# Softmax minus one-hot on one core: which queue issues the stores of the second rows

## The chip, the cores and the metric

The kernel runs on one core of a Trainium2 chip. The core has five engines with instruction streams of their own: TensorE (PE), VectorE (DVE), ScalarE (ACT), GpSimd (POOL) and SyncE (SP). They meet at semaphores. Data move between HBM and the on-chip memory SBUF by DMAs, which an engine issues and sixteen DMA engines carry out. In this kernel SP and ACT issue DMAs. The profile calls SP's DMA queue q1 and ACT's q10, and marks issues by SPq and ACTq.

The metric is the device time of one execution in microseconds. An execution under the profiler gives a span, from the first to the last instruction, which is a little shorter than the time of a run.

## The reference

The kernel computes the gradient of a cross entropy with respect to the logits: the softmax of each row, minus one at the row's label. There are 8 x 1024 rows of 8192 float32.

```python
logits_max = np.max(logits, axis=-1, keepdims=True)
exp_logits = np.exp(logits - logits_max)
softmax = exp_logits / np.sum(exp_logits, axis=-1, keepdims=True)
...
one_hot[batch_idx, seq_idx, labels] = 1.0
return (softmax - one_hot).astype(np.float32)
```

The logits are read once and the output is written once, 268 MB each way.

## The kernel before

The 8192 rows are cut into 32 blocks of 256. A block holds two rows on each of the 128 partitions (G = 2): partition p has the rows 2p and 2p + 1 of its block, beside each other in memory. In what follows "a row" is the tile of 128 partitions x 8192 float32, one row of each partition. So there are 64 rows, t = 0 to 63; t0 is the first and t1 the second row of a block b, and j = t mod 2 says which one it is. SBUF holds three blocks (SLOTS = 3), each with both rows in place: a row is loaded, worked on where it lies, and stored from there. Block b + 3 goes into the slot of block b.

Each row passes through these steps:

- `load(b)` (lines 101 to 112). The string `LOADS` says in what pieces: blocks 0 to 2 in half tiles ("s"), blocks 3, 4 and 29 to 31 by row ("r"), and blocks 5 to 28 in one piece with both rows ("w"). Each piece waits for the stores of the rows whose place it takes. All loads are issued by SP, but for one half of the pieces of blocks 0 to 2, which ACT issues.
- `row_max(t)`: VectorE takes the negated maximum (TENSOR_REDUCE).
- `exponentials(t)`: ACT computes the exponentials in place and their sum (ACTIVATE X<-X,m).
- `mark(t)`: ACT writes the one-hot of the row as bytes into `hot`, in PSUM, with two activations. `hot` has room for two rows, so the marker of row t + 2 waits until row t is finished (`freed`).
- `finish(t)`: VectorE takes the reciprocal of the sum, then scales the row and subtracts the one-hot bytes, in place (SCALAR_TENSOR_TENSOR).
- `store(t)` (lines 114 to 133): the finished row goes to HBM. `STORES` has "r" for all blocks: one DMA of 4 MB for each row. The last two rows go in halves, the first of them from SP and the second from ACT (lines 117 to 124).

The order of the work is written out by hand in the loop at the end (lines 244 to 279), and each engine runs its instructions in that order. For block b it is: the maximum of t1, finish t0, exponentials of t1, store t0, marker of t0 + 2; then the maximum of the next block's first row, finish t1, exponentials of the next first row, store t1, marker of t1 + 2, and at last `load(b + 3)`. So on ACT's stream the store of a row stands between the exponentials of the row after it and a marker, and waits there for VectorE's `finished[t]`. On SP's stream there is nothing behind the first loads but further loads and, at the very end, the halves of row 62. An engine's stream goes on once a DMA is issued; it doesn't stop until the data have landed, but a wait in it holds back all that stands behind.

All instructions are recorded by the helper `run` (lines 71 to 82), which sets all waits but the last as instructions of their own (line 75) and the last one on the instruction itself. Line 76 is therefore the line of nearly all instructions in the profile, and rows are told apart by engine, operation and tile. A one-piece load waits at line 75 for the store of its slot's first row, and at line 76 for that of the second.

Of the kernel before, what the change touches and what calls it, by code (L numbers as in the profile page):

```python
# [9 lines left out]
SLOTS = 3  # L10
# [7 lines left out]
def kernel(  # L18
# [6 lines left out]
    nc = tc.nc  # L25
# [38 lines left out]
    with tc.tile_critical():  # L64
        sem = tc.alloc_semaphore
        got = [[sem(f"got{i}{q}") for q in range(4)] for i in range(SLOTS)]
        put = [[sem(f"put{i}{q}") for q in range(4)] for i in range(SLOTS)]
# [3 lines left out]
        def run(engine, waits, counter, method, **operands):  # L71

            waits = list(dict.fromkeys(waits))
            for w in waits[:-1]:
                engine.wait_ge(*w)  # L75
            instruction = getattr(engine, method)(**operands)  # L76
            for w in waits[-1:]:
                instruction._wait_ge(*w)
            step = 16 if method == "dma_start" else 1
            instruction.then_inc(counter, step)  # L80
            count[counter.name] = count.get(counter.name, 0) + step
            return counter, count[counter.name]
# [16 lines left out]
        maxed, summed, marked, finished, freed = {}, {}, {}, {}, {}  # L99
# [14 lines left out]
        def store(t):  # L114
            b, j = divmod(t, G)
            stored.setdefault(b, [])
            if t >= T - G:
                for i, cs in enumerate(sides):
                    w = run(
                        nc.sync if t == T - G else nc.scalar, [sides_done[t][i]], put[b % SLOTS][G * j + i],  # L120
                        "dma_start", out=o_b[b, every, one[j], cs], in_=X[every, b % SLOTS, one[j], cs],
                    )
                    stored[b].append(((every, one[j]), w))
                return
            for q, piece in enumerate(PIECES[STORES[b]]):
                ps, js = piece
                if js.stop != j + 1:
                    continue
                w = run(
                    nc.scalar, [finished[t]], put[b % SLOTS][q], "dma_start",  # L130
                    out=o_b[b, ps, js, :], in_=X[ps, b % SLOTS, js, :],
                )
                stored[b].append((piece, w))
# [110 lines left out]
        for b in range(B):  # L244
            t0, t1 = b * G, b * G + 1
            nxt = t1 + 1
            if ORDER[b] == "b":
                if t0 not in maxed:
                    row_max(t0)
                    exponentials(t0)  # L250
                row_max(t1)
                exponentials(t1)
                finish(t0)
                store(t0)
                mark(t0 + G)
                finish(t1)
                store(t1)
                mark(t1 + G)
                if b + SLOTS < B:
                    load(b + SLOTS)  # L260
                continue
# [4 lines left out]
            finish(t0)  # L266
            exponentials(t1)
            store(t0)
            mark(t0 + G)
            ahead = nxt < T and ORDER[b + 1] == "r"  # L270
# [42 lines left out]
```

## Time and profile before

| what | value |
|---|---|
| time of a run, median of 3 | 1248.87 us (1248.83 to 1249.43) |
| span of the profiled execution | 1246.6 us |
| VectorE busy | 1120.2 us, 90% |
| ACT busy | 722.7 us, 58% |
| DMA queues, share of the sixteen engines' span | 51.5% (q10) and 48.3% (q1) |
| HBM read, written | 268.50 MB, 268.44 MB |

Views of the profile are used as follows. The page gives the busy time of each engine, the DMA queues (packets, MB, share of the sixteen engines' span) and the DMA issues (size, and the median us from issue to landing). The waits tell who waited for whom (us in total, times, longest). The chain of waits is followed back from the end of the program, in order of time (start us, us, what). The timeline has start, duration, engine, line, operation, output<-input; a duration with "x2" spans from the first to the last of two instructions, and what stands in brackets is the idle time before it and what ended it. A row of a table by stretches has start:end, length, the busy time of PE, PEld, DVE, ACT and POOL, then PE's clock, the DMA share and GB/s. The DMA view may be limited to a stretch; its packets count where they start, and its issues carry their own time to landing.

### The profile page before, as it was taken

Reading aid. Unit: us, or ns where it says so; the run is one execution under the profiler, and the core shown is the slowest. Engines: PE = TensorE matmul, PEld = TensorE weight load, DVE = VectorE, ACT = ScalarE, POOL = GpSimd, SP = SyncE. Lnnn points to the kernel's source line nnn. Section 1 sums busy time; section 2 is a strip of 40 time slices with the busy share of each in tenths; the row PEclk is TensorE's granted clock in tenths of the full one; section 3 lists DMA queues with packets and bytes.
Section 4 is the critical chain, followed back from the end, with each engine's and each line's share of the span. In section 5 each row is a group of like instructions: output and inputs, shape, how many; then the busy total and the mean of one; then the engine's idle time right before and its main releaser. Section 6 shows DMA issues by size and latency. Waiting matters only on the chain.

```text
span 1246.6 us, 809 instructions
## 1 busy us (share of the span) xinstructions
PE 0.4 (0%) x2; PEld 0.3 (0%) x2; DVE 1120.2 (90%) x208; ACT 722.7 (58%) x257; POOL 2.3 (0%) x7
## 2 busy tenths in 40 slices
PE   0000000000000000000000000000000000000000
PEld 0000000000000000000000000000000000000000
DVE  5999998889988889888898888998889988899995
ACT  2866664556555565465655655556556555566662
POOL 0000000000000000000000000000000000000000
DMA  9999999999999999999999999999999999999998
GB/s 406 413 431 434 437 432 444 435 437 421 433 429 437 443 423 433 434 431 435 430 441 435 422 435 435 434 440 426 432 434 431 433 446 434 422 430 435 429 434 383
DMA packets 15413, 536.98 MB, mean 431 GB/s; under 512 B 1808, under 2 KB 1808, under 8 KB 1840
## 3 DMA queue, kind: packets, MB, share of 16 engines
q10 hardware_dynamic: 9744, 276.89, 51.5%
q1 hardware_dynamic: 5664, 260.05, 48.3%
q14 instruction: 5, 0.04, 0.0%
HBM read 268.50 MB, written 268.44 MB: 431 GB/s over the span
## 4 chain that ended last, share of the span: by engine, by line
DMA 59%; DVE 26%; issue 11%; ACT 3%; DVEq 0%; ACTq 0%; SPq 0%
DMA X<-in_logits_dram 33%; DMA out_dram<-X 26%; DVE X L76 15%; DVE m L76 10%; ACT X L76 2%; DVEq L64 0%; DVE r L76 0%; ACT hot L76 0%; ACT away L76 0%; ACTq L76 0%; DVEq L75 0%; ACTq L308 0%; SPq L64 0%
## 5 line engine op out<-in xcount | busy, mean ns | idle before, releaser
L76 ACT ACTIVATE X<-X,m 128x8192 f32<-128x8192 f32 x64 | 455.8, 7122 | 365.2 <-DVE m L76 365.2
L76 DVE TENSOR_REDUCE m<-X 128x1 f32<-128x8192 f32 x64 | 555.6, 8682 | 105.4 <-DMA X<-in_logits_dram 105.4
L76 DVE SCALAR_TENSOR_TENSOR X<-X,r,hot 128x8192 f32<-128x8192 f32 (+1 forms) x66 | 560.1, 8489 | 3.8 <-ACT hot L76 1.6
L76 ACT ACTIVATE away<-count,word 128x2048 bf16<-128x2048 int16 x64 | 128.1, 2001 | 127.0 <-DVE X L76 127.0
L76 ACT ACTIVATE hot<-away,unit,minus 128x2048 int32<-128x2048 bf16 x64 | 131.9, 2061 | 2.1
L76 ACT ACTIVATION_READ_ACCUMULATOR X<-X,m 128x1 f32 x64 | 11.9, 186 | 0.0
L76 DVE RECIPROCAL r<-s 128x1 f32<-128x1 f32 x64 | 9.8, 153 | 0.0
L76 ACT ACT_TABLE_LOAD x1 | 1.3, 1283 | 5.3 <-issue 5.3
L76 DVE CAST lab_f<-lab_raw 32x256 f32<-32x256 int32 x1 | 0.5, 536 | 2.7 <-DMA lab_raw<-in_labels_dram 2.7
L76 POOL IOTA count<- 128x2048 int16 x1 | 1.8, 1823 | 0.0
L76 DVE TENSOR_TENSOR unit<-unit,part 128x64 f32<-128x64 f32 x3 | 0.7, 225 | 0.1
L76 DVE CAST lab<-hot 128x64 int32<-128x64 f32 x1 | 0.2, 224 | 0.5 <-PE hot L76 0.5
L76 DVE TENSOR_SCALAR part<-minus 128x64 f32<-128x64 f32 x3 | 0.6, 194 | 0.1
L76 PE MATMUL hot<-ident,lab_f 32*128 32x32 f32 x2 | 0.4, 298 | 3.3 <-DVE lab_f L76 3.3
L76 PEld LDWEIGHTS hot<-ident,lab_f 32*128 32x128 f32 x2 | 0.3, 192 | 3.3 <-DVE lab_f L76 3.3
L76 DVE CAST minus<-lab 128x64 f32<-128x64 int32 x1 | 0.2, 195 | 0.0
L76 DVE TENSOR_SCALAR word<-part 128x64 f32<-128x64 int32 x1 | 0.2, 195 | 0.0
L76 DVE TENSOR_SCALAR lab<-lab 128x64 int32<-128x64 int32 x1 | 0.2, 195 | 0.0
L76 DVE TENSOR_SCALAR unit<-minus 128x64 f32<-128x64 f32 x1 | 0.2, 195 | 0.0
L76 DVE TENSOR_SCALAR part<-lab 128x64 int32<-128x64 int32 x1 | 0.2, 194 | 0.0
L76 DVE TENSOR_SCALAR minus<-unit 128x64 f32<-128x64 f32 x1 | 0.2, 194 | 0.0
L76 POOL TENSOR_SCALAR_AFFINE_SELECT ident<-ident 32x32 f32<-32x32 f32 x1 | 0.2, 203 | 0.1
(5 smaller groups left out, 0.5 us busy)
## 6 DMA issues: line engine op xcount, KB each, us to landing
out_dram<-X ACTq DMA_DIRECT2D x62, 4096.0 KB, 30.4
X<-in_logits_dram SPq DMA_DIRECT2D x10, 4096.0 KB, 28.1
X<-in_logits_dram SPq DMA_DIRECT2D x6, 2048.0 KB, 32.6
X<-in_logits_dram ACTq DMA_DIRECT2D x6, 2048.0 KB, 37.1
out_dram<-X SPq DMA_DIRECT2D x2, 2048.0 KB, 12.7
out_dram<-X ACTq DMA_DIRECT2D x2, 2048.0 KB, 11.9
X<-in_logits_dram SPq DMA_DIRECT2D x24, 33.4
lab_raw<-in_labels_dram ACTq DMA_DIRECT2D x1, 64.0 KB, 1.8
```

What stands on the lines that cost most here:

```text
L76: instruction = getattr(engine, method)(**operands)
```

## The change

The stores of second rows (j = 1) of the blocks 0 to 30 are issued by SP in place of ACT. In SP's stream they stand where `store(t1)` is called, which is just ahead of the call of `load(b + 3)`. The stores of first rows stay with ACT, and the halves of the last two rows stay where they were. Waits, sizes, semaphores and the order of all else are the same.

```diff
                 w = run(
-                    nc.scalar, [finished[t]], put[b % SLOTS][q], "dma_start",
+                    nc.sync if j else nc.scalar, [finished[t]], put[b % SLOTS][q], "dma_start",
                     out=o_b[b, ps, js, :], in_=X[ps, b % SLOTS, js, :],
                 )
```

## The prediction

> Names: L(b) is the load of block b, F(b) the store of its first row (j = 0), S(b) the store of its second row (j = 1). A row is 128 x 8192 f32, 4.19 MB; a load in one piece ("w", blocks 5 to 28) is 8.39 MB.
>
> **What bounds the kernel now.** I read the page first, for engines and DMA.
>
> ```profile
> span 1246.6 us, 809 instructions
> PE 0.4 (0%) x2; PEld 0.3 (0%) x2; DVE 1120.2 (90%) x208; ACT 722.7 (58%) x257; POOL 2.3 (0%) x7
> ...
> q10 hardware_dynamic: 9744, 276.89, 51.5%
> q1 hardware_dynamic: 5664, 260.05, 48.3%
> ...
> out_dram<-X ACTq DMA_DIRECT2D x62, 4096.0 KB, 30.4
> ...
> X<-in_logits_dram SPq DMA_DIRECT2D x24, 33.4
> lab_raw<-in_labels_dram ACTq DMA_DIRECT2D x1, 64.0 KB, 1.8
> ```
>
> VectorE is busy 90%, but the two DMA queues (q1 is SP's, q10 ACT's) fill 51.5 + 48.3 = 99.8% of the sixteen engines' time. 536.9 MB in 0.998 x 1246.6 = 1244 us is 0.4316 MB a us: a row takes 9.72 us of the whole DMA, a one-piece load 19.44. A block (two rows in, two out) takes 38.9 us. No shorter time than about 1244 is to be had without moving fewer bytes, and any moment in which both queues are empty is added to the end. So I look only for such moments. By stretches, then by waits:
>
> ```profile
> 198.70:1050.80 852.10, 0.00 (x0) 0.00 (x0) 767.10 (x133) 496.21 (x176) 0.00 (x0) 1.00 1.00 433
> 1050.80:1246.60 195.80, 0.00 (x0) 0.00 (x0) 178.28 (x34) 108.71 (x38) 0.00 (x0) 1.00 0.99 425
> ```
>
> ```profile
> DVE m L76 <- DMA X<-in_logits_dram: 105.4, 26, 8.9
> ...
> SPq L75 <- DMA out_dram<-X: 511.1, 24, 21.6
> ```
>
> The first stretch runs from the issue of L(6) to that of L(28): 22 periods in 852.1 us, 38.73 each, DMA share 1.00 (next to last number). VectorE waits for loads, 105.4 us in all, and SP waits 24 times at line 75 for a store: once for each one-piece load. The chain of waits and the timeline give one period:
>
> ```profile
> 482.00 26.58 DMA out_dram<-X
> ...
> 508.59 33.63 DMA X<-in_logits_dram
> ...
> 559.82 26.10 DMA out_dram<-X
> ...
> 585.94 33.61 DMA X<-in_logits_dram
> ```
>
> ```profile
> 503.58 8.69 DVE L76 TENSOR_REDUCE m<-X 128x1 f32<-128x8192 f32 x1 [4.16 <-DMA X<-in_logits_dram]
> 508.59 38.99 SPq L76 DMA_DIRECT2D X<-in_logits_dram  x2
> 512.37 8.75 DVE L76 SCALAR_TENSOR_TENSOR X<-X,r,hot 128x8192 f32<-128x8192 f32 x1
> 521.15 0.34 ACTq L76 DMA_DIRECT2D out_dram<-X  x1
> 529.82 8.75 DVE L76 SCALAR_TENSOR_TENSOR X<-X,r,hot 128x8192 f32<-128x8192 f32 x1
> 538.60 0.34 ACTq L76 DMA_DIRECT2D out_dram<-X  x1
> 542.25 8.69 DVE L76 TENSOR_REDUCE m<-X 128x1 f32<-128x8192 f32 x1 [3.69 <-DMA X<-in_logits_dram]
> ```
>
> Call the landing of a load A (503.6 here). VectorE then takes the maximum of the new block's first row and finishes the block before it: S is issued at A + 17.6 (521.15), F of the new block at A + 35.0 (538.60). Then VectorE waits for the next landing (542.25). An S takes 26.6 us to land, and its landing releases a load (482.00 + 26.58 = 508.58, issue 508.59). The point to see is what the DMA does between landings:
>
> ```profile
> q1 hardware_dynamic: 144, 8.39, 61.3%
> q10 hardware_dynamic: 178, 5.31, 38.8%
> ```
>
> ```profile
> q10 hardware_dynamic: 81, 2.13, 100.8%
> ```
>
> The first fence is the stretch 510.5 to 542.2: the load moves 8.39 MB, the stores beside it 5.31. The second is 542.3 to 547.2, from the load's last packets to the next load's issue: q10 alone fills the engines. ACT's queue still holds S, with F (538.60) behind it, when S lands and while the next load starts. That backlog is what hides the turn from store to load.
>
> **The change part by part.** *On ACT:* 31 second-row stores go (blocks 0 to 30), 31 x 0.34 = 10.5 us of issue. ACT is busy 58% and the marker behind each store waits for the same VectorE instruction, so I count nothing.
>
> *On SP, the waits:* S(k) stands in front of L(k+3). SP reaches it when L(k+2) is out, waits for VectorE, issues, and goes on to wait for S(k) to land, as it did before. L(k+3) needs S(k) anyway, so the added wait holds up no one-piece load. The row-wise loads (blocks 3, 4, 29 to 31) could start on their first row earlier than S is issued; for them S is queued in front and streams first, so the engines have work and I count nothing.
>
> *On the rings:* this is where the time changes. S(k) now lies in SP's queue behind L(k+2), in order, and ACT's queue holds F alone. Take the landing of L(k+2) as A. At A the queue goes over to S(k); F(k+1) is issued a little before A. Packets of stores are equal (178 for 5.31 MB on q10, some of them completions of no size), so S and F share evenly, and two rows take 2 x 9.72 = 19.4 us. F started no later, so it is done first or at the same time. S lands at about A + 19.4. Now both queues are empty: the next S is at best issued by SP behind the load it has yet to issue, and the next F comes 35 us after A. SP issues L(k+3), which runs alone for 19.4 us. The period is 19.4 + gap + 19.4: the old 38.7 plus the gap.
>
> *The gap* is the landing of the store, the issue of the load, and the time until its packets run on idle engines. No row of before has this turn, so I bound it. The two ends are DMAs issued at the start, on empty engines: the labels' (last row of the first fence) and the first piece of L(0), here the traffic up to its landing and its issue:
>
> ```profile
> DMA packets 150, 3.28 MB, mean 349 GB/s; under 512 B 20, under 2 KB 20, under 8 KB 52
> ...
> q1 hardware_dynamic: 68, 2.10, 58.3%
> q10 hardware_dynamic: 82, 1.18, 29.6%
> ```
>
> ```profile
> X<-in_logits_dram SPq DMA_DIRECT2D x1, 2048.0 KB, 9.9
> ```
>
> The labels: 1.8 us for 0.064 MB, of which 0.15 is data, leaves 1.65. The first load piece on SP: 9.9 us from issue (0.96) to landing. Until then (0.95 to 10.35) the engines moved 3.28 MB, without the labels 3.22, which is 7.5 us of data; 2.4 is left. This is the fixed part of a DMA from issue to landing, and a chain store, load, store pays it once at each turn. I take 2.4, since that DMA is SP's own load with large packets. The dearer end is the start of a load while the other queue runs (508.6 to 512.0, just behind an issue):
>
> ```profile
> q10 hardware_dynamic: 40, 1.31, 89.2%
> ...
> X<-in_logits_dram SPq DMA_DIRECT2D x1, 33.6
> ```
>
> In 3.4 us not one packet of q1 has begun. On engines that have run empty there is nothing to stand behind, so I keep 3.4 as the upper end only. The lower end is 0: F may cover the gap.
>
> The Trainium skill (DMA: Bandwidth & Descriptors, section "Anatomy of one DMA") gives a DMA a fixed cost of about 2.0 us, mostly the receipt of the last write; by it the sum below would be 23 x 2.0 = 46 us instead of 55.
>
> *Does F cover it?* F is issued at 35.0 after its block's landing. At a period of 41.1 that is 6.1 before the next landing, more than the 3.4 that a queue needed to get its turn beside the other one, so F runs when S begins, and S is the last to end. At 38.7 F would be issued only 3.7 before (538.60 to 542.25): too close to call. Once a gap has opened, F is issued earlier still against the landing, and the gap stays.
>
> *How many gaps:* one for each one-piece load, 24. The first, L(5), falls where VectorE has not yet waited long for a load, so first-row stores still come every 35 us without regard to landings and one is likely queued:
>
> ```profile
> 149.25 0.34 ACTq L76 DMA_DIRECT2D out_dram<-X  x1
> ...
> 184.15 0.34 ACTq L76 DMA_DIRECT2D out_dram<-X  x1
> 192.52 8.69 DVE L76 TENSOR_REDUCE m<-X 128x1 f32<-128x8192 f32 x1 [8.41 <-DMA X<-in_logits_dram]
> ```
>
> I count 23. Behind L(28) the loads come in rows: the first row of the next one waits for an F that landed long before, and is queued right behind S, so no gap opens; that stretch, at 0.99 now, stays full.
>
> **The sum.** 23 x 2.4 = 55 us on the profiled 1246.6 gives 1301.8. The median of the runs shown, 1248.87, lies 2.3 above that span, so the forecast is **1304**. With VectorE's wait: 3.7 becomes about 6.1 a period, and at 35.0 us a block VectorE does not take over.
>
> **Rivals.** *(1) The queue does not matter* (not slower). The same bytes run on the same engines; F gets its turn late and is still running when S lands, so the load's start is hidden as now. It decides at 3.4 us: if F is issued less than the time a queue needs for its turn before the load's end, S is ahead by up to two packets on each engine and F outlasts it. For it: 3.7 against 3.4, and load packets, twice as large (144 packets, 16 of them completions, for 8.39 MB), may hold an engine longer. Against: one late turn on one of sixteen engines opens a gap, which then feeds itself. Time: 1246.6 + 2.3 = 1249.
> The Trainium skill speaks for this one (same page, section "Issuing engines are not separate DMA queues"): DMAs of SP and ACT run on the same engines and interleave, and the choice of issuer only saves time on the issuing sequencer. The fences above agree that both queues share the engines (61.3 and 38.8%).
>
> *(2) Half covered.* S is ahead by one packet, and F outlasts it by that: 178 - 16 = 162 packets for 5.31 MB are 0.0328 MB each, on one of sixteen engines 0.0328 / (0.4316 / 16) = 1.2 us. Gap 2.4 - 1.2: 23 x 1.2 = 28, 1276. F's turn would have to come at 4 to 6 us.
>
> *(3) A dear start.* If the 3.4 us belong to any queue that has run empty, the gap is 3.4 and some landing time, say 3.6: 23 x 3.6 = 83, 1332. Against it: the labels' whole trip of 1.8.
>
> *(4) The load keeps its 33.6 us* although it now follows S strictly: the period is 19.4 + 2.4 + 33.6 = 55.4, 23 x 16.7 = 384, 1633. Against it: 33.6 came from sharing (5.31 MB beside it).
>
> *(5) Faster:* at best the 0.2% of DMA time that is idle now, 2.5 us: 1246.
>
> **How the numbers follow.** Forecast 62%, (1) 12, (2) 15, (3) 8, (4) 1, (5) 2. About 0.2% (2.5 us) is what a measurement of this kernel can tell from no change: faster 0.02, same 0.11, slower 0.87. The forecast alone, with the gap at 1.65 to 2.8 (the landings of sixteen engines may spread further), covers 23 x 1.65 = 38 to 23 x 2.8 = 64: 1287 to 1313. The range reaches down past (2), to some blocks covered and some not (13 us), and up nearly to (3): 1262 to 1330.
>
> **What would show it.** DMA share in the middle stretch from 1.00 to 0.94, and 433 GB/s to about 409; period 41.1. One-piece loads land in about 19.4 + 2.4 = 22 us instead of 33.4. S, on SP, lands some 40 us after issue (behind a whole load), F on ACT in about 6 + 18 = 24 to 26 instead of 30.4. VectorE's wait for loads goes to about 160 us. A period of 38.7 with q10 packets in the turn proves (1); a gap of 3 us or more with empty engines proves (3).

## The result and the profile after

The changed kernel takes 1344.16 us (median of 5 runs, 1340.84 to 1346.43) against 1248.83 us for the kernel before, measured beside it (5 runs, 1248.63 to 1249.43): a ratio of 1.0761, 95% interval 1.0748 to 1.0773. It is slower by 95 us, where 55 were forecast, and 14 us above the upper end of the range. The direction and the place were right; the price of one turn was not.

The page of the profiled execution (span; busy time of the engines; DMA queues with packets, MB and share of the sixteen engines' span; DMA issues with the median us to landing):

```profile
span 1340.1 us, 809 instructions
PE 0.4 (0%) x2; PEld 0.3 (0%) x2; DVE 1120.2 (84%) x208; ACT 722.7 (54%) x257; POOL 2.3 (0%) x7
...
q1 hardware_dynamic: 10128, 390.07, 70.7%
q10 hardware_dynamic: 5280, 146.87, 25.5%
...
out_dram<-X ACTq DMA_DIRECT2D x31, 4096.0 KB, 24.5
out_dram<-X SPq DMA_DIRECT2D x31, 4096.0 KB, 42.1
...
X<-in_logits_dram SPq DMA_DIRECT2D x24, 24.4
```

VectorE and ACT do the same work in the same busy time. The queues fill 70.7 + 25.5 = 96.2% of the engines' time, where it was 99.8%. This alone splits the loss into two nearly equal parts, and only the first of them was foreseen. Idle time of the DMA engines: 3.8% of 1340.1 is 51 us, against 0.2% of 1246.6, 2.5 us before: 48 us more. Time that packets took: 0.962 x 1340.1 = 1289 us against 1244, for the same 537 MB: 45 us more. Packets became longer.

By stretches, cut at the issues of L(6) and L(28) (start:end, length, busy time of PE, PEld, DVE, ACT, POOL, then PE's clock, DMA share, GB/s):

```profile
212.60:1150.00 937.40, 0.00 (x0) 0.00 (x0) 769.34 (x134) 496.63 (x177) 0.00 (x0) 1.00 0.95 394
1150.00:1340.10 190.10, 0.00 (x0) 0.00 (x0) 165.44 (x31) 101.05 (x36) 0.00 (x0) 1.00 0.98 419
```

The 22 periods between these issues take 42.6 us each, 3.9 more than the 38.73 before; that is 85 of the 93.5 us by which the span grew. Two more turns lie outside this stretch, that of L(5) ahead of it and that of L(28) behind it, and 24 x 3.9 = 93.5. The waits (us in total, times, longest us) and one period in the timeline:

```profile
DVE m L76 <- DMA X<-in_logits_dram: 196.9, 27, 11.4
...
SPq L76 <- DMA out_dram<-X: 1154.0, 32, 42.5
```

```profile
364.06 8.69 DVE L76 TENSOR_REDUCE m<-X 128x1 f32<-128x8192 f32 x1 [7.25 <-DMA X<-in_logits_dram]
372.86 8.75 DVE L76 SCALAR_TENSOR_TENSOR X<-X,r,hot 128x8192 f32<-128x8192 f32 x1
...
382.21 0.33 SPq L76 DMA_DIRECT2D X<-in_logits_dram  x1
382.58 0.43 SPq L76 DMA_DIRECT2D out_dram<-X  x1
...
399.09 0.34 ACTq L76 DMA_DIRECT2D out_dram<-X  x1
406.75 8.69 DVE L76 TENSOR_REDUCE m<-X 128x1 f32<-128x8192 f32 x1 [7.70 <-DMA X<-in_logits_dram]
...
424.89 0.33 SPq L76 DMA_DIRECT2D X<-in_logits_dram  x1
```

SP issues a load (382.21), right behind it the second-row store, which VectorE has finished just before (372.86 + 8.75), and then waits for the landing of that store, 42.3 us, to issue the next load (424.89). The first-row store goes out at 399.09, 7.7 us before the next load lands. Now the same stretch in the DMA view; each digit is the busy share of a slice of 0.25 us in tenths. The busy time of a packet, like its bytes, is put down in the slice where the packet starts, so a 0 behind a row of 9s doesn't mean an idle engine. First 378 to 388, from the end of the second-row store into the load; then 396 to 406, from the load into the stores:

```profile
DMA  9003990099900000000099907000000069906000
GB/s 918 0 0 131 1049 918 0 0 393 1180 524 0 0 0 0 0 0 0 0 0 1311 1835 786 0 262 0 0 0 0 0 0 0 262 1573 2097 0 262 0 0 0
```

```profile
DMA  9960000009996000009990900000000099933999
GB/s 2359 1049 262 0 0 0 0 0 0 786 2359 786 262 0 0 0 0 0 262 1573 2097 0 262 0 0 0 0 0 0 0 0 0 393 786 655 131 131 393 918 655
```

One sees rounds of sixteen packets, one on each engine. In the first view the last packets of the store start at about 380.5 and the first ones of the load at 383.3. A store packet takes 1.2 us, so the engines stand empty for some 1.6 us by these slices. By the packet records of the trace (start, length, size and queue of each packet) an engine is empty for 1.8 us on average in this turn and for 2.1 over all 24. The first load packets need about 3.0 us to the next round (383.3 to 386.4); inside a load it is 2.4. In the second view rounds of the load start at 398.5 and 400.9 (2.4 us), and the first packets of the stores at 404.3, 3.4 us later: the last round of the load took a microsecond too long. In a window of 1 us that holds just one round of a load, the share of q1 reads as the mean length of a packet (100% is 1 us). Here are the first round of this load (window 383.1 to 384.1), one from its middle (393.4 to 394.4) and the last (400.7 to 401.7):

```profile
q1 hardware_dynamic: 16, 1.05, 315.6%
```

```profile
q1 hardware_dynamic: 16, 1.05, 241.9%
```

```profile
q1 hardware_dynamic: 16, 1.05, 345.5%
```

In these longer rounds no engine counts as idle. Over the 22 loads of the middle stretch the first round averages 3.11 us, the last 3.55, and the six between them 2.42 to 2.43, while store packets keep their 1.21 us. So 1.8 us a period are longer packets of the load, and 2.1 + 1.8 = 3.9 is the whole excess. The longer packets are the half of the loss that the prediction does not have.

### The profile page after: what moved, and what is told of

Same layout as the page of the kernel before. It is cut to its first block, busy times and chain, and to the rows that moved or that the text cites. A ratio compares the mean times of both kernels' runs of the same rounds, so it can differ in the third digit from the quotient of the medians.

```text
span 1340.1 us, 809 instructions
## 1 busy us (share of the span) xinstructions
PE 0.4 (0%) x2; PEld 0.3 (0%) x2; DVE 1120.2 (84%) x208; ACT 722.7 (54%) x257; POOL 2.3 (0%) x7
## 3 DMA queue, kind: packets, MB, share of 16 engines
q1 hardware_dynamic: 10128, 390.07, 70.7%
q10 hardware_dynamic: 5280, 146.87, 25.5%
## 4 chain that ended last, share of the span: by engine, by line
DMA 82%; DVE 10%; issue 3%; ACT 2%; SPq 1%; DVEq 0%; ACTq 0%
DMA out_dram<-X 74%; DMA X<-in_logits_dram 8%; DVE m L76 5%; DVE X L76 5%; ACT X L76 2%; SPq L76 1%; DVEq L64 0%; ACT hot L76 0%; ACT away L76 0%; DVE r L76 0%; ACTq L76 0%; DVEq L75 0%; ACTq L308 0%; SPq L64 0%
## 5 line engine op out<-in xcount | busy, mean ns | idle before, releaser
L76 DVE TENSOR_REDUCE m<-X 128x1 f32<-128x8192 f32 x64 | 555.6, 8682 | 196.9 <-DMA X<-in_logits_dram 196.9
## 6 DMA issues: line engine op xcount, KB each, us to landing
out_dram<-X ACTq DMA_DIRECT2D x31, 4096.0 KB, 24.5
out_dram<-X SPq DMA_DIRECT2D x31, 4096.0 KB, 42.1
X<-in_logits_dram SPq DMA_DIRECT2D x24, 24.4
```

## The experiments

For each run the two parts are taken from its page as above: shares of the queues times the span is the packet time, the rest is idle. Before, they are 1244 and 2.5 us, with the change 1289 and 51.

**Both stores on SP.** Does the lengthening at the load's end come from ACT's first-row store, which gets its turn just there?

```diff
-                    nc.sync if j else nc.scalar, [finished[t]], put[b % SLOTS][q], "dma_start",
+                    nc.sync, [finished[t]], put[b % SLOTS][q], "dma_start",
```

> Both stores of a block on SP; ACT's queue is empty after the first loads. Theory A (the loss is the turns of SP's queue: store to load on empty engines, about 2.8 us with its landing, and load to store within one queue, about 1.1 us, whatever ACT does): the period stays at 42 to 43 us, 1340 to 1350 us in all. Theory B (the 1.1 us at the end of a load come from the late first packets of the first-row store on ACT's queue, 5.1 us after its issue): without that store the period falls to about 41.4, some 24 x 1.1 = 26 us less than the changed kernel, 1318.

Measured: 1341.39 us, ratio to the kernel before 1.0746 (1.0730 to 1.0762). Packets 1289 us, idle 51: the same as with the change. The chain of waits (start us, us, what) keeps the period:

```profile
629.45 0.34 SPq L76
...
671.94 0.34 SPq L76
```

42.5 us from load to load. Theory B falls: without the stores of these blocks on ACT's queue the loss is the same. Shares of 93.2 (q1) and 3.0% (q10) also show that one queue can carry nearly the whole traffic; what it can't do is go past its own waits.

**Loads by row.** With the change, a load of a first row need not wait for the second-row store that lies ahead of it in SP's queue.

```diff
-LOADS = "sssrrwwwwwwwwwwwwwwwwwwwwwwwwrrr"
+LOADS = "sssrrrrrrrrrrrrrrrrrrrrrrrrrrrrr"
```

> The changed kernel with all loads from block 3 on by row. The load of a first row then waits only for a first-row store that landed long before, and lies in SP's queue right behind the second-row store. Theory A: no moment with both queues empty is left, 1249 to 1256. If the turn from load to store within SP's queue costs 1.1 us also with the engines supplied, 29 x 1.1 = 32 more, about 1281. Rival (a store that must pass behind a load in one queue is slow in itself, whatever follows it): it stays near 1340.

Measured: 1270.92 us, ratio 1.0186 (1.0164 to 1.0207). The second-row store still lies on SP's queue behind a load, takes 39.1 us to land, and yet three quarters of the loss are gone: idle falls from 51 to 6 us. What costs the idle time is the empty queue behind the store, not the place behind the load. The remaining 23 us lie between the two ends that were expected, 1256 and 1281; most of them are longer packets (1261 us, 17 more than before). The same edit to the kernel before:

> The kernel before with all loads from block 3 on by row: the counterpart of the changed kernel with loads by row (1270.9). If loads by row cost nothing in themselves, as the DMA is busy 99.8% either way: 1248 to 1252, and then some 20 us of the 1270.9 belong to the change, through the turns left in SP's queue. If the loads by row cost the 20 us: near 1270.

Measured: 1248.63 us, ratio 1.0002 (0.9993 to 1.0011), so loads by row cost nothing in themselves. The middle stretch with and without the change:

```profile
209.00:1120.00 911.00, 0.00 (x0) 0.00 (x0) 808.22 (x141) 520.58 (x185) 0.00 (x0) 1.00 1.00 427
```

```profile
209.00:1120.00 911.00, 0.00 (x0) 0.00 (x0) 829.85 (x144) 536.10 (x189) 0.00 (x0) 1.00 1.00 433
```

The first row is the changed kernel with loads by row, the second the kernel before with them. Both have a DMA share of 1.00, but 427 against 433 GB/s: a busy DMA that moves less.

**Twelve one-piece loads.** Is it a price for each turn, or a rhythm that is entered once?

```diff
-LOADS = "sssrrwwwwwwwwwwwwwwwwwwwwwwwwrrr"
+LOADS = "sssrrwwwwwwwwwwwwrrrrrrrrrrrrrrr"
```

> The changed kernel with twelve one-piece loads (blocks 5 to 16) in place of 24, the rest by row. All 24 cost 1344.2 - 1248.8 = 95 us, none cost 1270.9 - 1248.0 = 23. If the price is one and the same for each one-piece load followed by row loads: half way, about 1307. Rival (a price paid once, on entry into a worse rhythm that lasts to the end): near 1344.

Measured: 1307.24 us, ratio 1.0476 (1.0456 to 1.0496). Half the loads, half the way: a price for each one-piece load. Packets 1275 us and idle 31 lie half way too.

**A third queue.** The second-row stores leave ACT, but not for SP's queue.

```diff
-        put = [[sem(f"put{i}{q}") for q in range(4)] for i in range(SLOTS)]
+        put = [[sem(f"put{i}{q}") for q in range(5)] for i in range(SLOTS)]
...
-                    nc.sync if j else nc.scalar, [finished[t]], put[b % SLOTS][q], "dma_start",
+                    nc.gpsimd if j else nc.scalar, [finished[t]], put[b % SLOTS][4 if j else q], "dma_start",
```

> The second-row stores are issued by GpSimd, on a third queue, with a semaphore of their own. Theory A (what costs is that the store lies in order behind the load in SP's queue): it runs beside the load again and the time is 1249 to 1260. Rival (what costs is that ACT's queue has only the first-row stores, so that there is no backlog at the turn): still above 1300, since a third queue gives ACT no backlog.

Measured: 1285.97 us, ratio 1.0293 (1.0270 to 1.0315): between the two, and at first sight against theory A. By stretches, and in the chain of waits:

```profile
248.80:1120.00 871.20, 0.00 (x0) 0.00 (x0) 774.04 (x133) 500.26 (x178) 11.69 (x22) 1.00 1.00 426
0.00:248.80 248.80, 0.42 (x2) 0.28 (x2) 203.66 (x49) 136.32 (x49) 5.11 (x12) 1.00 0.97 405
1120.00:1289.00 169.00, 0.00 (x0) 0.00 (x0) 142.84 (x28) 86.15 (x30) 2.12 (x4) 1.00 0.93 386
```

```profile
533.58 31.50 DMA X<-in_logits_dram
...
611.05 31.61 DMA X<-in_logits_dram
```

These two issues are two blocks apart: 38.7 us a period, as before the change. That is the best part of the run: from the load at 376.08 to the one at 1083.01 eighteen blocks take 39.3 us each. The second-row stores are off ACT's queue, as in the change, and yet the steady rhythm comes within 0.6 us of the old one, as the store doesn't lie in SP's queue, and the middle stretch has no idle time (share 1.00). That part of theory A holds, but not its time of 1249 to 1260. By the page packets take 1270 us, 26 more than before, and idle is 19 us, mainly at the start and the end (shares 0.97 and 0.93). Why GpSimd's queue costs this was not followed up.

**First-row stores later.** The prediction says that the turn is bare since the first-row store is done too early. Then issuing it later must make the kernel faster.

```diff
+                late = [w for _, w in loaded.get(b + 1, [])] if j == 0 and LOADS[b] == "w" else []
                 w = run(
-                    nc.sync if j else nc.scalar, [finished[t]], put[b % SLOTS][q], "dma_start",
+                    nc.sync if j else nc.scalar, [finished[t]] + late, put[b % SLOTS][q], "dma_start",
```

> The changed kernel, but in blocks 5 to 28 ACT issues the first-row store only when the next block's load has landed, about 6 us later than in the changed kernel. Theory A (both queues are empty at the turn because the first-row store is done before the second-row store): it now starts some 4 to 5 us behind and outlasts the second-row store by 3 to 5 us, which covers the turn to the load; 1249 + 24 x (0 to 1.5) = 1249 to 1285, faster than the changed kernel by over 60 us although a store is issued later. If it leaves the turn from load to store uncovered, 24 x 1.1 = 26 stay, 1275. Rival (each store issued later costs its delay): 1344 and more.

Measured: 1301.61 us, ratio 1.0423 (1.0407 to 1.0438): 43 us faster than the changed kernel through a delayed store, though 17 us more than the upper end that was expected. In its chain two blocks lie between these loads:

```profile
615.43 24.88 DMA X<-in_logits_dram
...
696.30 24.50 DMA X<-in_logits_dram
```

40.4 us a period. Idle falls from 51 to 17 us, so the cover works for most of the empty time; packets stay at 1282 us. The late store starts beside the second-row store and not beside the end of the load, and the last round of a load still averages 3.38 us.

**First-row stores beside the end of the load.** Is the long last round tied to the turn inside SP's queue, and does other traffic hide it? Here a first-row store is issued one block later, at the maximum of the next block's second row.

```diff
             row_max(t1)
+            if 3 <= b - 1 <= 27:
+                store(t0 - G, [maxed[t1]])
+                load_late(b - 1)
             finish(t0)
             exponentials(t1)
-            store(t0)
+            if not 3 <= b <= 27:
+                store(t0)
             mark(t0 + G)
...
-            if b + SLOTS < B:
-                load(b + SLOTS)
+            if not 3 <= b <= 27:
+                load_late(b)
```

The second argument of `store` adds waits, and `load_late(b)` is the old call of `load(b + SLOTS)` with its condition. On SP the order of stores and loads stays.

> The changed kernel, but in blocks 3 to 27 ACT issues the first-row store one block later, once VectorE has the maximum of the next block's second row: some 10 us before the end of the load in flight. Its packets then run on both sides of the turn from load to second-row store, and it is done long before that store. Theory A (each turn of SP's queue costs only where ACT's queue has nothing running): the 1.1 us at the load's end go, the 2.5 us and more between store and load stay: about 1344 - 24 x 1.1 = 1318. Rival (load to store in one queue stops the engine whatever else runs): 1344. If the later store pays its delay: above 1344.

Measured: 1342.74 us, ratio 1.0748 (1.0730 to 1.0767). Nothing came back, as the rival says, but not for its reason. The DMA view of 636 to 646, in slices of 0.25 us, where ACT's store enters while the load goes on for another ten microseconds (SP's second-row store begins near 656.5):

```profile
DMA  6000000999000000099900000000099930099600
...
q1 hardware_dynamic: 49, 3.21, 84.9%
q10 hardware_dynamic: 13, 0.43, 9.9%
```

Rounds start near 638.1 and 640.5, 2.4 us apart, all of the load. The next round, the first with store packets of q10, starts at about 643.5: 3.0 us. The loss moved with the store to its new place: over the middle stretch the fifth and sixth rounds of a load, where the store enters, average 2.79 and 3.11 us (on some engines it enters behind the fifth, on others behind the sixth), and the last round, just ahead of SP's store, has 2.42. So here the loss isn't tied to the turn inside SP's queue, nor to the load's end: it comes where a store enters a stream in which the engines had only loads, from whichever queue. Packets 1286, idle 55.

**Halves at both turns.** Half of the first-row store is issued when the next load lands, as in the late run, the other half as in the run just told.

```diff
+                store(t0 - G, [maxed[t1]], (1,))
...
+                store(t0, [w for _, w in loaded[b + 1]], (0,))
```

> The changed kernel with the first-row stores of blocks 3 to 27 in two halves: the first half is issued when the next block's load has landed (it outlasts the second-row store and covers the turn to the next load), the second about 10 us before the end of the load in flight (it covers the turn from load to store). The second-row stores stay in SP's queue behind the loads, as in the change. Theory A: both turns are hidden, nearly all of the 95 us come back, 1249 to 1275. Rival (a second-row store in order behind a load costs its time whatever ACT does): 1300 and more, as with one turn covered (1301.6).

Measured: 1306.12 us (1294.82 to 1311.82), ratio 1.0451 (1.0391 to 1.0510). Idle is 18 us, packets 1281: the empty time is covered as in the late run, and long rounds remain. Theory A as it stood, that other traffic hides both turns, fails on the second. The rival's time came out. The packet records of the middle stretches tell the runs apart; this is the mean length in us of a load's rounds, of eight (those not listed have 2.42 to 2.49):

| run | first | fifth | sixth | last |
|---|---|---|---|---|
| kernel before | 2.45 | 2.42 | 2.42 | 2.42 |
| with the change | 3.11 | 2.42 | 2.42 | 3.55 |
| both stores on SP | 3.06 | 2.42 | 2.42 | 3.62 |
| first-row stores later | 2.95 | 2.43 | 2.42 | 3.38 |
| beside the end of the load | 3.06 | 2.79 | 3.11 | 2.42 |
| halves at both turns | 2.97 | 2.43 | 2.62 | 3.03 |

A whole store that enters before the end takes the loss away from the last round. A half store, which enters in the sixth, doesn't: the last round stays long although ACT's packets run beside it. So for the last run the rival isn't excluded, and why half a store differs from a whole one stays open.

**Smaller load packets.** With 64 bytes between rows in SBUF a one-piece load goes in packets of 32 KB; meant to bring ACT's store in before the load's end. Tried on both kernels.

```diff
-    X = const.tile([P, SLOTS, G, V], fp32)
+    X = const.tile([P, SLOTS, G, V + 16], fp32)
```

> The changed kernel with rows 64 bytes apart in SBUF, so that a one-piece load goes in packets of 32 KB in place of 64. Theory A: ACT's first-row store now gets its turn about 3.7 us after its issue in place of 5.1, that is, before the load ends; its packets then stand between the last packet of the load and the first of the second-row store, and hide that turn (1.1 us), while the turn from store to load stays open (2.5 us): 1344 - 24 x 1.1 = 1318, period 41.5. Rival (the turn from load to store in one queue stops the engine whatever else is queued): 1344.

> The kernel before with the same 64 bytes between rows. The DMA has no idle time to win, and stores now get half in place of a third of the engines beside a load: 1248 to 1252, which gives the run with smaller packets its own base.

Measured: 1350.57 us with the change (ratio 1.0821, 1.0798 to 1.0843) and 1268.37 without (ratio 1.0164, 1.0149 to 1.0179). The first says little: in its packet records ACT's store gets its turn some 4.5 us after issue, which is still at the load's end, so that the case meant to be made did not come about. The second was a miss and is instructive. The kernel before, with no store on SP, loses 20 us, 16 of them in longer packets (1260 us), though loads by row have packets of the same size and lose nothing. Its stores take an equal share beside a load and land sooner:

```profile
out_dram<-X ACTq DMA_DIRECT2D x62, 4096.0 KB, 22.4
```

22.4 us in place of 30.4, so ACT's queue runs dry beside a load before the next store comes: from 293.8 to 301.4, for one, no data of q10 move. That is again a load alone and then a store, here without any turn in SP's queue, and it fits what the store beside the load's end showed. It was seen in this one pair and not tried further.

## Why the prediction was wrong

*What bounds the kernel.* Right. The DMA sets the time: VectorE's busy time stayed at 1120.2 us, and its waits for loads grew by 91.5 us (105.4 to 196.9) while the span grew by 93.5.

*ACT's part and SP's waits.* Right: ACT's busy time is the same, and the by-row loads behind L(28) open no new gaps: in the packet records the last turn with empty engines is that of L(28), at 1151. (The stretch from its issue on takes 190.1 us against 195.8, but it also has less left to move, 79.7 MB against 83.2.)

*The order on the rings.* Right, and shown. The store behind the load takes 42.1 us to land, the load alone 24.4, the first-row store 24.5 (forecast: about 40, 22, and 24 to 26). The third queue brings back a period of 38.7 to 39.3, the by-row loads take the idle time from 51 to 6 us, the late first-row stores to 17.

*The gap of 2.4 us.* Near: the engines are empty for 2.1 us in a turn, and 24 x 2.1 = 50 us where 23 x 2.4 = 55 were counted. In part that is luck. The 2.4 came from a load piece at the start that landed at 10.86, but its traffic was taken only up to 10.35; by 10.86 packets of 3.74 MB in place of 3.28 had started, and the same sum would have left 1.4. The Trainium skill gives a fixed cost of about 2.0 us for a DMA that GpSimd issues (DMA: Bandwidth & Descriptors, section "Anatomy of one DMA"). The 2.1 us of empty engines in this turn of SP's queue lie near that figure. No gap of this size accounts for the 3.9.

*The step that failed* is "The period is 19.4 + gap + 19.4: the old 38.7 plus the gap." It takes rows at the rate of the mixed stream, 9.72 us each, also where loads run alone and where a store enters behind them. In the changed kernel that entry costs the last round of the load about 1.1 us, once a period, and the first round on empty engines is longer by 0.7. Together this makes the 45 us of longer packets, half of the loss. The signs named for the middle stretch tell it: DMA share 0.94 was forecast and 0.95 measured, but 409 GB/s and a period of 41.1 were forecast where 394 and 42.6 were measured. The price is a term that was left out: it showed nowhere in the middle stretch of before, because there a store ran beside nearly every load packet, and a rate read from such a stream says nothing of the first and the last round of a load alone. The rounds between them have the same 2.42 us as before. With the measured terms the sum closes: 2.1 of empty engines + 0.7 + 1.1 = 3.9 us a period.

*Does F cover it?* Right. F was issued 7.7 us before the landing (6.1 was forecast, at a shorter period) and was done when S landed. Rival (1), that the queue doesn't matter, is refuted. By the sentence of the Trainium skill that stood beside it (DMA: Bandwidth & Descriptors, section "Issuing engines are not separate DMA queues"), the choice of the issuing engine only saves issue time; for this change that does not hold, as it cost 95 us. The engines are shared, but the choice of queue decides the order within it, with a wait for a landing in front of its next transfer. Rival (2) did not occur. Rival (3) named a price near the measured one (3.6) for a wrong reason: the load issued at 382.21 on empty engines has packets from 383.2 on, after 1.0 us and not 3.4.

*How many gaps.* 23 were counted, with the first thought covered. There are 24: the packet records show empty engines once behind the issue of each one-piece load, from L(5) (at 171, 1.9 us) to L(28) (at 1151, 2.0 us).

What stays open: what in a DMA engine makes the round long when a store enters a stream of loads. The runs show where it happens, and that it comes with stores on either queue, not why, nor why a half store leaves the last round long. Also open are the 23 us of the by-row loads with the change and GpSimd's loss.

No version tried beats the kernel before, whose DMA has 2.5 us of idle time left.

## What to carry to other kernels

Before a transfer is moved to another queue, write down that queue's transfers in order with the landing that each waits for, and ask at every such wait what the other queues still have in flight: where it is nothing, the engines stand empty for the landing, the issue and the start, each time (here 2.1 us). A rate taken from a stream of loads and stores mixed holds only while it stays mixed; where the change leaves one kind alone, its first and last packets need a price of their own, and if the profile has none, the range must be opened upwards. And read the share of busy DMA together with GB/s: half of this loss is in packets that count as busy.

## What the runs showed of the hardware

- Where a whole store entered a stream in which the engines had carried only loads, the load's round there became longer: with both stores on SP's queue the last round averages 3.62 us in place of 2.42, and with the store on ACT's queue in the midst of a load a round took 3.0 us (the store at 643.5). In the mixed stream of the kernel before, the rounds have 2.42 to 2.45 us, and the same bytes took 1244 us of packets in place of 1289.
- The first round of a load on empty engines averages 3.11 us in place of 2.42 (22 loads with the change).
- A load on empty engines had its first packets about 1.0 us after its issue (382.21 to 383.2); beside a running queue, in the kernel before, it had none in 3.4 us (508.6 to 512.0).
- A store held back on the other queue until the next load had landed made the kernel 43 us faster (1344.16 to 1301.61).
